# MLP of a decoder block: two sweeps, both by seven products, with weight sums made by accumulating DMA

## The chip, the core and the metric

The kernel runs on one core of a Trainium2 chip. The metric is the device time of one execution in microseconds (us). The kernel before was run three times; its median is the time that a changed kernel is held against.

## The reference

One decoder block on 512 rows of 2048 features: RMSNorm, a combined input projection, a gated delta rule and differential attention side by side, an output projection with a residual, and then the part that the change is about, the MLP, and a final RMSNorm:

```
h = h + mix @ w_o                                  # (512, 2048)
u = rms_norm(h, mlp_norm)
hid = square(relu(u @ w_up))                       # w_up (2048, 8192)
h = h + hid @ w_down                               # w_down (8192, 2048)
out = rms_norm(h, final_norm)
```

All inputs and the output are float32.

## The kernel before

Every large matrix product is made in fp32r by three matmuls: each operand is split into a rounded `hi` (ScalarE, line 147) and the rest `lo` (VectorE, line 149), and hi x hi, hi x lo and lo x hi are accumulated in PSUM. `parts` does this for a weight tile of 128 x 1024 that `load_w` has brought into a slot; slots come from pools by tag, so many for each (`BUFS`, line 43: six `raw`, three `hi`, three `lo`). All loads go through SP's queue in the order of the program. The Tile framework orders the instructions of each engine and sets the semaphores; each engine then takes its queue in order.

The MLP starts at line 947. The hidden width of 8192 is cut into 16 blocks of 512 (`NBLK`). `to_feature_major` makes the split, transposed activations `uT`: 16 tiles of 128 features x 512 rows. `up_first` makes the first block's hidden values, `up_steps` those of each later block, in four column tiles, with 512-column matmuls (`cols_steps`, lines 204 to 206); `squared_relu` writes them.

The down projection of a block is made by seven products instead of eight (a scheme of Winograd's kind): the block's hidden values, 512 x 512, and each 512 x 1024 piece of `w_down` are cut into four quarters. `seven_steps` makes the seven factors of the hidden values from sums and differences of quarters and splits each with `two`. `block_steps` goes over two column halves `p`; in each it loads four quarters of `w_down`, makes four combinations of them on VectorE (lines 864, 870, 878, 884), splits seven tiles, runs seven products (`product`, lines 835 to 837: 12 matmuls of 512 columns each, into two PSUM banks) and adds banks into the rows of h (lines 850, 852), which stay in SBUF all the time. The last block is done without the scheme (`plain_steps`).

The loop at line 996 weaves three streams: the down products of block b, the up projection of blocks b + 1 and b + 2, and the factors of block b + 1. So 360 matmuls belong to one turn, 192 up and 168 down.

Of the kernel before, what the change touches and what calls it, by code (L numbers as in the profile page):

```python
# [31 lines left out]
def hybrid_block(ctx: ExitStack, tc: tile.TileContext, x, attn_norm, w_in, conv_w, a_log, dt_bias,  # L32
# [10 lines left out]
    BUFS = {"p": 10, "x": 2, "w": 8, "m": 2, "u": 16, "raw": 6, "hi": 3, "lo": 3}  # L43
# [750 lines left out]
    def half_tile():  # L794

        return big("p", [P, 2, 2, 256], nm="hf")

    def two(src):
        z = big("w", [P, 2, 2, 256], F32R, nm="op")
        A.activation(z[:, 0], src, AF.Copy)  # L800
        V.tensor_sub(z[:, 1], src, z[:, 0].bitcast(F32))
        return z[:, 0], z[:, 1]

    def seven_steps(left, f):

        a11, a21, a12, a22 = left[0][:, 0], left[0][:, 1], left[1][:, 0], left[1][:, 1]
        f["a12"] = two(a12)
        yield
        f["a11"] = two(a11)
        z = big("m", [P, 2, 2, 256], nm="s12")  # L810
        s1, s2 = z[:, 0], z[:, 1]
        V.tensor_add(s1, a21, a22)
        yield
        f["s1"] = two(s1)
        V.tensor_sub(s2, s1, a11)
        yield
        f["s2"] = two(s2)
        s4 = s1
        V.tensor_sub(s4, a12, s2)
        yield  # L820
        f["s4"] = two(s4)
        s3 = s2
        V.tensor_sub(s3, a11, a21)
        yield
        f["s3"] = two(s3)
        yield
        f["a22"] = two(a22)
        yield

    def product(bank, fac, wts, first, last_):  # L830
        (ah, al), (bh, bl) = fac, wts
        for k in range(2):
            for t in range(2):
                st = slice(t * P, (t + 1) * P)
                T.matmul(bank[t], lhsT=ah[:, k, st], rhs=bh[:, k, :], start=first and k == 0, stop=False, skip_group_check=True)  # L835
                T.matmul(bank[t], lhsT=ah[:, k, st], rhs=bl[:, k, :], start=False, stop=False, skip_group_check=True)  # L836
                T.matmul(bank[t], lhsT=al[:, k, st], rhs=bh[:, k, :], start=False, stop=last_ and k == 1, skip_group_check=True)  # L837

    def block_steps(f, w, row0, rows):

        for p in range(2):
            def quarter(i, j):
                r0, c0 = row0 + 256 * i, 1024 * j + 512 * p
                return load_w(w[r0:r0 + 256, c0:c0 + 512].rearrange("(k p) n -> p k n", p=P), [P, 2, 512])

            def add(bank, half, cg, op=ALU.add):
                for t in range(2):
                    dst = rows[2 * half + t][cg]
                    if op == ALU.add:
                        V.tensor_add(dst, bank[t], dst)  # L850
                    else:
                        V.tensor_sub(dst, dst, bank[t])

            b21, b11, b12, b22 = quarter(1, 0), quarter(0, 0), quarter(0, 1), quarter(1, 1)
            Y = [bank(), bank()]
            product(Y, f["a12"], parts(b21, 2), True, True)
            add(Y, 0, p)
            yield
            X = [acc(), acc()]
            product(X, f["a11"], parts(b11, 2), True, False)  # L860
            add(X, 0, p)
            yield
            t1 = b11
            V.tensor_sub(t1, b12, b11)
            Z = [acc(), acc()]
            product(Z, f["s1"], parts(t1, 2), True, False)
            add(Z, 1, p + 2)
            yield
            t2 = t1
            V.tensor_sub(t2, b22, t1)  # L870
            product(X, f["s2"], parts(t2, 2), False, False)
            add(X, 0, p + 2)
            yield
            product(Z, f["s4"], parts(b22, 2), False, True)
            add(Z, 0, p + 2)
            yield
            t3 = b12
            V.tensor_sub(t3, b22, b12)
            product(X, f["s3"], parts(t3, 2), False, True)
            add(X, 1, p)  # L880
            add(X, 1, p + 2)
            yield
            t4 = b21
            V.tensor_sub(t4, t2, b21)
            Y = [bank(), bank()]
            product(Y, f["a22"], parts(t4, 2), True, True)
            add(Y, 1, p, ALU.subtract)
            yield
# [57 lines left out]

    def up_unit(u):
        return split(w_up[0, u * 256:(u + 1) * 256, 0:512].rearrange("(k p) n -> p k n", p=P), [P, 2, 512])
# [3 lines left out]
    uT = to_feature_major(h, rstd, g_mlp)  # L952
    NBLK = DFF // 512

    def up_steps(b, j, left):
        z = half_tile()
        for k in range(2):
            po = sps()
            yield from cols_steps(po, w_up[0], (4 * b + 2 * j + k) * P, uT, tag="x")
            squared_relu(z, k, po)  # L960
        left.append(z)

    def squared_relu(z, k, po):
        r = big("m", [P, 512], nm="relu")
        A.activation(r, po, AF.Relu)
        A.activation(z[:, :, k, :], r.rearrange("p (i s) -> p i s", i=2), AF.Square)

    def up_first():

        po = [acc() for _ in range(4)]  # L970
        for u in range(KD // 2):
            hi, lo = up_unit(u) if u else first
            for j in range(2):
                k = 2 * u + j
                ah, al = uT[k]
                for c in range(4):
                    st = slice(c * P, (c + 1) * P)
                    T.matmul(po[c], lhsT=hi[:, j, st], rhs=ah, start=k == 0, stop=False)
                    T.matmul(po[c], lhsT=hi[:, j, st], rhs=al, start=False, stop=False)
                    T.matmul(po[c], lhsT=lo[:, j, st], rhs=ah, start=False, stop=k == KD - 1)  # L980
        for j in range(2):
            z = half_tile()
            for k in range(2):
                squared_relu(z, k, po[2 * j + k])
            lefts[0].append(z)

    def up(b, j):
        return up_steps(b, j, lefts[b]) if b < NBLK else iter(())

    lefts = [[] for _ in range(NBLK)]  # L990
    facs = [{} for _ in range(NBLK)]
    up_first()
    floor.clear()
    run(seven_steps(lefts[0], facs[0]))
    run(up(1, 0))
    for b in range(NBLK - 2):
        down = block_steps(facs[b], w_down[0], 512 * b, h)
        for p in range(2):
            ups = up(b + 1, 1) if p == 0 else up(b + 2, 0)
            fac = seven_steps(lefts[b + 1], facs[b + 1]) if p == 1 else iter(())  # L1000
            for i in range(7):
                next(down)
                next(fac, None)
                if i % 2 == 0:
                    next(ups, None)
            run(ups)


    down = block_steps(facs[NBLK - 2], w_down[0], 512 * (NBLK - 2), h)
    ups = up(NBLK - 1, 1)  # L1010
    for i in range(7):
        next(down)
        if i % 2 == 0:
            next(ups, None)
    run(ups)
    lft = lefts[NBLK - 1]
# [94 lines left out]
```

## Time and profile before

| | |
|---|---|
| median of three runs | 2282.1 us (2281.64 to 2282.75) |
| profiled execution, its own time | 2282.81 us |
| span of the profiled execution | 2281.1 us |
| granted TensorE clock, mean | 0.997 |
| PE / weight loads / VectorE / ScalarE / POOL busy | 98% / 82% / 67% / 39% / 2% |
| DMA moved | 249.67 MB, mean 109 GB/s |
| first MLP matmul, last part | about 956 us to 2273 us from the span's start |

The profile is of one execution, and its span is the time from the first to the last instruction on the core; the time of that execution is 1.7 us more. Matmuls overlap, so the duration in a matmul's row is longer than the step from one start to the next.

### The profile page before, as it was taken

How to read it: one execution, taken by the hardware profiler on the slowest of the kernel's cores; microseconds unless marked ns; L12 is line 12 of the kernel's file. 1: busy time of each engine (PE TensorE's matmuls, PEld its weight loads, DVE VectorE, ACT ScalarE, POOL GpSimd, SP SyncE). 2: the span in 40 equal slices, each digit the busy share in tenths (PEclk: the TensorE clock that was granted, in tenths of full speed). 3: DMA queues.
4: the chain of work that ended last, by engine and by line, in shares of the span. 5: the costliest groups of instructions: out<-in, count | busy, mean ns of one | idle time of the engine just before them, and what ended most of it. 6: DMA issues, size and time to landing. Idle time of an engine off the chain costs nothing.

```text
span 2281.1 us, 27449 instructions
## 1 busy us (share of the span) xinstructions
PE 2245.4 (98%) x10649; PEld 1864.8 (82%) x10649; DVE 1523.3 (67%) x2338; ACT 887.8 (39%) x1444; POOL 55.5 (2%) x85
## 2 busy tenths in 40 slices
PE   8999999999999999999999999999999999999998
PEld 7988777778888788788888888888888888888887
DVE  5467787863355623437787687777778778777776
ACT  5233434432344523433344343343334334434343
POOL 0000100100000000000000000000000000000000
PEclk9999999999999999999999999999999999999999
DMA  8433333433232434233333333232332333323332
GB/s 282 141 111 95 109 97 96 117 92 110 85 95 88 139 92 151 83 105 98 109 93 119 95 99 113 93 123 90 98 115 93 115 98 95 118 93 120 93 127 95
DMA packets 288570, 249.67 MB, mean 109 GB/s; under 512 B 17300, under 2 KB 229560, under 8 KB 288440
## 3 DMA queue, kind: packets, MB, share of 16 engines
q1 hardware_dynamic: 287952, 247.72, 35.3%
q8 instruction: 83, 1.36, 0.3%
q14 instruction: 47, 0.39, 0.1%
q10 hardware_dynamic: 488, 0.21, 0.0%
HBM read 236.86 MB, written 11.03 MB: 109 GB/s over the span
## 4 chain that ended last, share of the span: by engine, by line
PE 90%; DVE 7%; ACT 1%; issue 1%; DMA 1%; POOL 0%; SPq 0%; ACTq 0%; POOLq 0%; DVEq 0%
PE s L206 10%; PE s L204 10%; PE s L205 10%; PE acc L837 6%; PE acc L836 6%; PE acc L835 6%; PE acc L204 5%; PE acc L205 4%; PE acc L206 4%; PE acc L220 3%; PE acc L221 3%; PE acc L222 3%; PE s L837 2%; PE s L836 2%; PE s L835 2%; DVE X L520 2%
## 5 line engine op out<-in xcount | busy, mean ns | idle before, releaser
L149 DVE TENSOR_TENSOR lo<-raw,hi 128x1024 fp32r<-128x1024 f32 (+2 forms) x370 | 443.9, 1200 | 342.3 <-ACT hi L147 337.5
L147 ACT ACTIVATE hi<-raw 128x1024 fp32r<-128x1024 f32 (+2 forms) x370 | 384.5, 1040 | 674.5 <-PE acc L205 136.7
L204 PE MATMUL s<-u,hi 128*128 128x512 f32 x960 | 373.4, 389 | 0.0
L205 PE MATMUL s<-u,hi 128*128 128x512 f32 x960 | 373.4, 389 | 0.0
L206 PE MATMUL s<-u,lo 128*128 128x512 f32 x960 | 373.4, 389 | 0.0
L149 DVE TENSOR_TENSOR lo<-x,hi 128x1024 fp32r<-128x1024 f32 x120 | 146.7, 1223 | 181.0 <-ACT hi L147 181.0
L204 PE MATMUL acc<-u,hi 128*128 128x512 f32 x640 | 260.6, 407 | 0.8 <-DVE dvl L679 0.6
L205 PE MATMUL acc<-u,hi 128*128 128x512 f32 x640 | 251.6, 393 | 0.0
L206 PE MATMUL acc<-u,lo 128*128 128x512 f32 x640 | 250.7, 392 | 0.0
L147 ACT ACTIVATE hi<-x 128x1024 fp32r<-128x1024 f32 x120 | 127.5, 1062 | 315.0 <-PE s L205 226.2
L836 PE MATMUL acc<-lo,op 128*128 128x512 f32 x600 | 233.4, 389 | 0.0
L837 PE MATMUL acc<-hi,op 128*128 128x512 f32 x600 | 233.4, 389 | 0.0
L835 PE MATMUL acc<-hi,op 128*128 128x512 f32 x600 | 233.1, 389 | 0.0
L850 DVE TENSOR_TENSOR h<-acc,h 128x512 f32<-128x512 f32 x360 | 232.2, 685 | 0.6 <-PE acc L837 0.5
L205 PEld LDWEIGHTS s<-u,hi 128*128 128x128 f32 x960 | 180.2, 188 | 37.4
L206 PEld LDWEIGHTS s<-u,lo 128*128 128x128 f32 x960 | 180.2, 188 | 37.4
L204 PEld LDWEIGHTS s<-u,hi 128*128 128x128 f32 x960 | 180.2, 188 | 37.4
L220 PE MATMUL acc<-hi,u 128*128 128x512 f32 (+2 forms) x384 | 144.7, 379 | 7.6 <-ACT hi L147 5.9
L204 PEld LDWEIGHTS acc<-u,hi 128*128 128x128 f32 x640 | 120.7, 189 | 25.0 <-DVE dvl L679 1.0
L206 PEld LDWEIGHTS acc<-u,lo 128*128 128x128 f32 x640 | 120.4, 188 | 25.3
L221 PE MATMUL acc<-lo,u 128*128 128x512 f32 (+2 forms) x384 | 140.5, 366 | 0.2 <-DVE lo L149 0.2
L222 PE MATMUL acc<-hi,u 128*128 128x512 f32 (+2 forms) x384 | 140.6, 366 | 0.0
(266 smaller groups left out, 3228.2 us busy)
## 6 DMA issues: line engine op xcount, KB each, us to landing
raw<-in_w_down_dram SPq DMA_DIRECT2D x128, 512.0 KB, 5.6
x<-in_w_up_dram SPq DMA_DIRECT2D x120, 512.0 KB, 4.2
raw<-in_w_in_dram SPq DMA_DIRECT2D x96, 512.0 KB, 3.9
raw<-in_w_o_dram SPq DMA_DIRECT2D x32, 512.0 KB, 3.8
raw<-in_w_in_dram SPq DMA_DIRECT2D x16, 384.0 KB, 8.3
w<-in_xt_dram SPq DMA_DIRECT2D x8, 512.0 KB, 8.5
p<-in_x_dram SPq DMA_DIRECT2D x8, 512.0 KB, 10.0
raw<-in_x_dram SPq DMA_DIRECT2D x8, 512.0 KB, 3.6
```

The lines of the kernel that those rows point to most:

```text
L147: A.activation(hi, raw, AF.Copy)
L149: floor["lo"] = V.tensor_sub(lo, raw, hi.bitcast(F32))
L204: T.matmul(po, lhsT=hi[:, j, :], rhs=ah, start=k == 0, stop=False)
L205: T.matmul(po, lhsT=hi[:, j, :], rhs=al, start=False, stop=False)
L206: T.matmul(po, lhsT=lo[:, j, :], rhs=ah, start=False, stop=k == KD - 1)
L220: T.matmul(o, lhsT=ah[:, st], rhs=bh, start=k == 0, stop=False)
L221: T.matmul(o, lhsT=ah[:, st], rhs=bl, start=False, stop=False)
L222: T.matmul(o, lhsT=al[:, st], rhs=bh, start=False, stop=k == KD - 1)
L835: T.matmul(bank[t], lhsT=ah[:, k, st], rhs=bh[:, k, :], start=first and k == 0, stop=False, skip_group_check=True)
L836: T.matmul(bank[t], lhsT=ah[:, k, st], rhs=bl[:, k, :], start=False, stop=False, skip_group_check=True)
L837: T.matmul(bank[t], lhsT=al[:, k, st], rhs=bh[:, k, :], start=False, stop=last_ and k == 1, skip_group_check=True)
L850: V.tensor_add(dst, bank[t], dst)
```

## The change

The MLP is made in two sweeps instead of one woven loop.

- **Up sweep.** Blocks 1 to 15 of the up projection are made by seven products too. The activations are cut in halves of rows (256) and of features (1024): `uh` holds the split tiles by halves, `uf` unsplit ones, and `u_factors` makes three of the seven factors in new tiles and a fourth in the place of the low half of `uh`. `up_product` takes 128 x 128 pieces of the weights as the stationary operand and 256 rows as the moving one: 48 matmuls of 256 columns for each product.
- **Factors by way of DRAM.** `seven_steps` makes the down projection's factors for each block as before, but `keep` stores each, split, in DRAM (512 KB), on SP's queue, for the last two blocks on POOL's. The rows of h are stored too (`hscr`) and brought back (`rows_back`).
- **Down sweep.** `block_steps` now handles a group of blocks, [0], [1 to 3], ..., [10 to 12], [13, 14], in one PSUM accumulation for each product, and adds into h once for a group. `recall` loads each factor once for a group, for both column halves.
- **Weight combinations.** The signs are moved to the factors, so that all four combinations of weights are sums. Two are made by VectorE (`sums`), two by `add_in`: a DMA issued from POOL that adds the quarter (0, 1) from DRAM onto a `raw` tile in SBUF, once it has been split for its first product.
- The tag `raw` has nine slots instead of six, and the scratch for dynamic DMA is 2048 instead of 1024.

The core of the diff (the functions taken out are those printed above):

```diff
-    BUFS = {"p": 10, "x": 2, "w": 8, "m": 2, "u": 16, "raw": 6, "hi": 3, "lo": 3}
+    BUFS = {"p": 10, "x": 2, "w": 8, "m": 2, "u": 16, "raw": 9, "hi": 3, "lo": 3}
...
+    def pair_of(src, tag):
+        z = big(tag, [P, 2, 2, 256], F32R, nm="op")
         A.activation(z[:, 0], src, AF.Copy)
         V.tensor_sub(z[:, 1], src, z[:, 0].bitcast(F32))
+        return z
+    fscr = {}
+    def keep(b, name, src):
+        z = pair_of(src, "w")
+        fscr[b, name] = dp.tile([P, 1024], F32, name=f"f_{name}_{b}")
+        E = nc.sync if b < NBLK - 2 else G
+        E.dma_start(out=fscr[b, name], in_=z.bitcast(F32).rearrange("p a k s -> p (a k s)"))
+    def negated_less(out, a, b):
+        V.scalar_tensor_tensor(out, a, -1.0, b, op0=ALU.mult, op1=ALU.subtract)
+    def seven_steps(b, left):
...
+        keep(b, "a11", a11)
+        yield
+        keep(b, "a12", a12)
+        V.tensor_sub(s1, a21, a22)
...
+        keep(b, "s3", s2)
+        yield
...
+    def recall(b, name):
+        z = big("w" if name in ("a12", "a22") else "u", [P, 2, 2, 256], F32R, nm="fac")
+        with tc.issue_after(last_load[0].ins):
+            last_load[0] = nc.sync.dma_start(out=z.bitcast(F32).rearrange("p a k s -> p (a k s)"), in_=fscr[b, name])
+        return z[:, 0], z[:, 1]
+    def add_in(raws, srcs, k):
+        for z, src in zip(raws, srcs):
+            G.dma_start(out=z.rearrange("p (k n) -> p k n", k=k), in_=src.rearrange("(k p) n -> p k n", p=P), accum_op=ALU.add)
+    def sums(a, b):
+        for x1, x2 in zip(a, b):
+            V.tensor_add(x1, x1, x2)
+    def product(bank, facs, wts, first, last_):
+        for n, ((ah, al), raw) in enumerate(zip(facs, wts)):
+            bh, bl = parts(raw, 2)
+            for k in range(2):
+                for t in range(2):
+                    st = slice(t * P, (t + 1) * P)
+                    head, tail = first and n == 0 and k == 0, last_ and n == len(facs) - 1 and k == 1
+                    T.matmul(bank[t], lhsT=ah[:, k, st], rhs=bh[:, k, :], start=head, stop=False, skip_group_check=True)
+                    T.matmul(bank[t], lhsT=ah[:, k, st], rhs=bl[:, k, :], start=False, stop=False, skip_group_check=True)
+                    T.matmul(bank[t], lhsT=al[:, k, st], rhs=bh[:, k, :], start=False, stop=tail, skip_group_check=True)
...
+        def quarter(i, j, tags=("raw",) * 3):
+            return [load_w(z.rearrange("(k p) n -> p k n", p=P), [P, 2, 512], tag=t) for z, t in zip(srcs(i, j), tags)]
...
+        t1 = quarter(0, 0)
+        fa = factor("a11")
+        X = [acc(), acc()]
+        product(X, fa, t1, True, False)
+        add_in(t1, srcs(0, 1), 2)
+        add(X, 0, p)
+        yield
+        b21 = quarter(1, 0, ("x", "x", "m"))
+        fa = factor("a12")
+        Y = [bank(), bank()]
+        product(Y, fa, b21, True, True)
+        add(Y, 0, p)
+        yield
+        fa = factor("s1")
+        Z = [acc(), acc()]
+        product(Z, fa, t1, True, False)
+        add(Z, 1, p + 2)
+        yield
+        t3 = quarter(1, 1)
+        fa = factor("s2")
+        sums(t1, t3)
+        product(X, fa, t1, False, False)
+        add(X, 0, p + 2, ALU.subtract)
+        yield
+        product(Z, factor("s4"), t3, False, True)
+        add_in(t3, srcs(0, 1), 2)
+        add(Z, 0, p + 2, ALU.subtract)
+        yield
+        fa = factor("s3")
+        product(X, fa, t3, False, True)
+        add(X, 1, p, ALU.subtract)
+        add(X, 1, p + 2)
+        yield
+        fa = factor("a22")
+        sums(t1, b21)
+        Y = [bank(), bank()]
+        product(Y, fa, t1, True, True)
+        add(Y, 1, p)
+        yield
...
+    uh, uf = [], [[], []]
...
+            z = big("u", [P, 2, 2, 256], F32R, nm="uh")
+            pv, sc = pt.rearrange("p (i s) -> p i s", i=2), g_mlp[:, k:k + 1]
+            A.activation(z[:, :, 0, :], pv, AF.Identity, scale=sc)
+            V.scalar_tensor_tensor(z[:, :, 1, :], pv, sc, z[:, :, 0, :].bitcast(F32), op0=ALU.mult, op1=ALU.subtract)
+            uh.append(z)
+            if k % 2 == 0:
+                uf[k // 8].append(big("w", [P, 2, 2, 256], nm="uf"))
+            A.activation(uf[k // 8][k % 8 // 2][:, k % 2], pv, AF.Identity, scale=sc)
+    for cg in range(4):
+        for t in range(NT):
+            G.dma_start(out=hscr[2 * cg + t // 2][:, t % 2, :], in_=h[t][cg])
...
+        floor.clear()
+        run(u_factors())
...
+    def u_factors():
+        for q in range(4):
+            xa, xb = uf[0][q], uf[1][q]
...
+            def put(n, src, tag):
+                o = big(tag, [P, 2, 2, 256], F32R, nm="u" + n)
+                A.activation(o[:, :, 0, :], src, AF.Copy)
+                V.tensor_sub(o[:, :, 1, :], src, o[:, :, 0, :].bitcast(F32))
+                for i in range(2):
+                    fu[n][2 * q + i] = o[:, i]
+            V.tensor_sub(s1, a21, a22)
+            put("s1", s1, "p")
+            negated_less(s2, s1, a11)
+            put("s2", s2, "p")
+            negated_less(s1, s2, a12)
+            put("s4", s1, "x" if q < 2 else "p")
+            V.tensor_add(a21, a11, a21)
+            for i in range(2):
+                k = 2 * q + i
+                fu["a11"][k], fu["a12"][k], fu["a22"][k] = uh[k][:, 0], uh[8 + k][:, 0], uh[8 + k][:, 1]
+                o = uh[k][:, 1]
+                A.activation(o[:, 0, :], a21[:, i, :], AF.Copy)
+                V.tensor_sub(o[:, 1, :], a21[:, i, :], o[:, 0, :].bitcast(F32))
+                fu["s3"][k] = o
+            yield
+    def up_product(bank, name, wts, first, last_):
+        for n, raw in enumerate(wts):
+            bh, bl = parts(raw, 4)
+            for j in range(4):
+                k = 4 * n + j
+                ah, al = fu[name][k][:, 0, :], fu[name][k][:, 1, :]
+                for c in range(2):
+                    dst, st = bank[:, c * 256:(c + 1) * 256], slice(c * P, (c + 1) * P)
+                    head, tail = first and k == 0 and c == 0, last_ and k == 7
+                    T.matmul(dst, lhsT=bh[:, j, st], rhs=ah, start=head, stop=False, skip_group_check=True)
+                    T.matmul(dst, lhsT=bh[:, j, st], rhs=al, start=False, stop=False, skip_group_check=True)
+                    T.matmul(dst, lhsT=bl[:, j, st], rhs=ah, start=False, stop=tail, skip_group_check=True)
+    def up_steps(b, left):
...
+            return [w_up[0, 1024 * i + 512 * n:1024 * i + 512 * n + 512, c0:c0 + 256] for n in range(2)]
+        def quarter(i, j):
+            return [load_w(z.rearrange("(k p) n -> p k n", p=P), [P, 4, 256]) for z in srcs(i, j)]
...
+        e1, e2 = (big("w", [P, 2, 512], nm="e") for _ in range(2))
+        x1, p5, u2, u3 = e1[:, 0, :], e1[:, 1, :], e2[:, 0, :], e2[:, 1, :]
+        t1 = quarter(0, 0)
+        X = acc()
+        up_product(X, "a11", t1, True, False)
+        add_in(t1, srcs(0, 1), 4)
+        A.activation(x1, X, AF.Copy)
+        yield
...
+        t3 = quarter(1, 1)
+        sums(t1, t3)
+        up_product(X, "s2", t1, False, False)
+        A.activation(u2, X, AF.Copy)
+        yield
+        up_product(Z, "s4", t3, False, True)
+        add_in(t3, srcs(0, 1), 4)
+        V.tensor_add(c12, Z, u2)
...
+        up_product(X, "s3", t3, False, True)
...
+        sums(t1, b21)
+        Y = bank()
+        up_product(Y, "a22", t1, True, True)
+        V.tensor_sub(c21, Y, u3)
...
+    left = up_first()
+    for b in range(1, NBLK):
+        fac, nxt = seven_steps(b - 1, left), []
+        for _ in up_steps(b, nxt):
+            next(fac, None)
+        run(fac)
+        left = nxt
+    last_fac = four_steps(NBLK - 1, left)
...
+    def rows_back(cgs):
+        for cg in cgs:
+            for i in range(2):
+                with tc.issue_after(last_load[0].ins):
+                    last_load[0] = nc.sync.dma_start(out=hb[2 * cg + i], in_=hscr[2 * cg + i])
+    groups = [[0]] + [[b, b + 1, b + 2] for b in range(1, NBLK - 3, 3)] + [[NBLK - 3, NBLK - 2]]
+    for g in groups:
+        f = {}
         for p in range(2):
+            down = block_steps(g, f, p, w_down[0], h)
+            if g is groups[0]:
+                rows_back((p, p + 2))
+            if g is groups[-1] and p == 1:
+                break
+            for _ in down:
+                next(last_fac, None)
...
-    nc = bacc.Bacc("TRN2", target_bir_lowering=False, num_devices=1, dynamic_dma_scratch_size=1024)
+    nc = bacc.Bacc("TRN2", target_bir_lowering=False, num_devices=1, dynamic_dma_scratch_size=2048)
```

## Rows read from the trace of the kernel before

**Rows 1.** The page's first part: busy us of each engine, share, instructions.
```profile
PE 2245.4 (98%) x10649; PEld 1864.8 (82%) x10649; DVE 1523.3 (67%) x2338; ACT 887.8 (39%) x1444; POOL 55.5 (2%) x85
```

**Rows 2.** Busy time by stretch, columns as its first line says.
```profile
core 0: us, PE busy (x) PEld busy (x) DVE busy (x) ACT busy (x) POOL busy (x), PEclk, DMA share, GB/s
2.00:30.00 28.00, 19.27 (x97) 18.58 (x98) 19.34 (x35) 18.75 (x31) 0.86 (x5) 1.00 0.99 349
966.00:1010.00 44.00, 44.00 (x196) 36.24 (x195) 15.51 (x16) 17.05 (x24) 0.00 (x0) 1.00 0.33 98
1300.00:1382.00 82.00, 82.00 (x363) 67.92 (x362) 61.60 (x73) 31.70 (x37) 0.00 (x0) 1.00 0.32 103
```

**Rows 3.** PE's waits over the whole span: us in total, times, longest.
```profile
PE acc L220 <- ACT hi L147: 5.9, 2, 4.5
PE s L114 <- DVE lp L112: 4.7, 1, 4.7
```

**Rows 4.** Timeline of PE, 512-column matmuls: start us, duration us, engine, line.
```profile
1500.12 0.39 PE L204 MATMUL s<-u,hi 128*128 128x512 f32 x1
...
1505.56 0.39 PE L835 MATMUL acc<-hi,op 128*128 128x512 f32 x1
```

**Rows 5.** Timeline of PE, 272-column matmuls.
```profile
84.77 0.29 PE L220 MATMUL acc<-hi,u 128*128 128x272 f32 x1
...
92.21 0.29 PE L222 MATMUL acc<-hi,u 128*128 128x272 f32 x1
```

**Rows 6.** Timeline of PE, 256-column matmuls.
```profile
646.74 0.28 PE L733 MATMUL s<-dvh,at 128*128 128x256 f32 x1
646.85 0.28 PE L734 MATMUL s<-dvl,at 128*128 128x256 f32 x1
646.97 0.28 PE L735 MATMUL s<-dvh,at 128*128 128x256 f32 x1
647.09 0.40 PE L220 MATMUL acc<-hi,u 128*128 128x512 f32 x1
```

**Rows 7.** Groups by line and shape on VectorE: count, busy us, mean ns.
```profile
L149 DVE TENSOR_TENSOR lo<-raw,hi 128x1024 fp32r<-128x1024 f32 x346 | 422.8, 1223 | 304.8 <-ACT hi L147 300.0 <-PE s L625 4.7
L850 DVE TENSOR_TENSOR h<-acc,h 128x512 f32<-128x512 f32 x360 | 232.2, 685 | 0.6 <-PE acc L837 0.5
L864 DVE TENSOR_TENSOR raw<-raw,raw 128x1024 f32<-128x1024 f32 x30 | 36.6, 1219 | 0.0
L801 DVE TENSOR_TENSOR op<-hf,op 128x512 fp32r<-128x512 f32 x49 | 32.3, 684 | 0.0
L812 DVE TENSOR_TENSOR s<-hf,hf 128x512 f32<-128x512 f32 x15 | 10.4, 692 | 0.0
```

**Rows 8.** The same on ScalarE.
```profile
L147 ACT ACTIVATE hi<-raw 128x1024 fp32r<-128x1024 f32 x346 | 365.7, 1058 | 629.7 <-PE acc L205 136.7 <-PE s L205 120.6 <-PE acc L837 116.3
L966 ACT ACTIVATE hf<-relu 128x512 f32<-128x512 f32 x64 | 40.4, 634 | 1.9
L965 ACT ACTIVATE relu<-s 128x512 f32<-128x512 f32 x60 | 34.7, 578 | 2.8 <-PE s L206 2.8
L800 ACT ACTIVATE op<-hf 128x512 fp32r<-128x512 f32 x49 | 30.9, 632 | 29.3 <-PE acc L837 27.7
```

**Rows 9.** DMA issues by line: count, KB each, median us from issue to landing.
```profile
raw<-in_w_down_dram SPq DMA_DIRECT2D x128, 512.0 KB, 5.6
x<-in_w_up_dram SPq DMA_DIRECT2D x120, 512.0 KB, 4.2
p<-in_x_dram SPq DMA_DIRECT2D x8, 512.0 KB, 10.0
raw<-in_x_dram SPq DMA_DIRECT2D x8, 512.0 KB, 3.6
```

**Rows 10.** Groups by line and shape on POOL.
```profile
L128 POOL TENSOR_TENSOR rstd<-rs,mhalf 128x1 f32<-128x1 f32 x24 | 13.7, 571 | 1644.2 <-DVE rs L127 1644.2
L128 POOL TENSOR_TENSOR fac<-rs,mhalf 128x8 f32<-128x8 f32 x4 | 8.0, 1993 | 144.2 <-DVE rs L127 144.2
```

More of the change, by code (lines that the diff above doesn't have):

```diff
@@ L822, in seven_steps @@
-        s3 = s2
-        V.tensor_sub(s3, a11, a21)
+        keep(b, "s2", s2)
         yield
-        f["s3"] = two(s3)
+        negated_less(s1, s2, a12)
+        keep(b, "s4", s1)
         yield
-        f["a22"] = two(a22)
+        keep(b, "a22", a22)
+        V.tensor_add(s2, a11, a21)
         yield
-    def product(bank, fac, wts, first, last_):
-        (ah, al), (bh, bl) = fac, wts
-        for k in range(2):
-            for t in range(2):
[L834 to L888, printed above, removed]
@@ new lines, in seven_steps, with four_steps @@
+        keep(b, "s3", s2)
+        yield
+    def four_steps(b, left):
+        for j in range(2):
+            for i in range(2):
+                keep(b, f"a{i + 1}{j + 1}", left[j][:, i])
+                yield
[4 more added lines that the diff above has]
+        return z[:, 0], z[:, 1]
@@ new lines, in block_steps, with srcs, factor, add @@
+    def block_steps(bs, f, p, w, rows):
+        def srcs(i, j):
+            c0 = 1024 * j + 512 * p
+            return [w[512 * b + 256 * i:512 * b + 256 * i + 256, c0:c0 + 512] for b in bs]
+        def quarter(i, j, tags=("raw",) * 3):
+            return [load_w(z.rearrange("(k p) n -> p k n", p=P), [P, 2, 512], tag=t) for z, t in zip(srcs(i, j), tags)]
+        def factor(name):
+            if name not in f:
+                f[name] = [recall(b, name) for b in bs]
+            return f[name]
+        def add(bank, half, cg, op=ALU.add):
+            for t in range(2):
+                dst = rows[2 * half + t][cg]
+                if op == ALU.add:
+                    V.tensor_add(dst, bank[t], dst)
+                else:
+                    V.tensor_sub(dst, dst, bank[t])
+        t1 = quarter(0, 0)
[37 more added lines that the diff above has]
+        yield
@@ L944, in hybrid_block @@
     run(rows_steps(po, w_o[0], 3 * 512, 512, mix, by_token=4, done=finish))
+    NBLK = DFF // 512
     def up_unit(u):
@@ L974, in up_first @@
                 k = 2 * u + j
-                ah, al = uT[k]
+                ah, al = uh[k][:, :, 0, :], uh[k][:, :, 1, :]
                 for c in range(4):
@@ L983, in up_first @@
             for k in range(2):
[L984 to L997, printed above, removed]
-        for p in range(2):
[L999 to L1006, printed above, removed]
@@ L1009, in hybrid_block @@
[L1009 to L1016, printed above, removed]
-    fac = [[two(lft[j][:, i]) for i in range(2)] for j in range(2)]
+                r = big("m", [P, 512], nm="relu")
+                A.activation(r, po[2 * j + k], AF.Relu)
+                A.activation(z[:, :, k, :], r.rearrange("p (i s) -> p i s", i=2), AF.Square)
```

95 lines of the change are left out of this document (65 added, 30 removed).

## Prediction

> **What bounds the kernel now.** I read the page's part 1 first, then the same kind of figures for single stretches, then the waits of TensorE, then the rows of single matmuls, and last the prices of what the other engines and the DMA queues do.
>
> The page's first part [rows 1] says that PE is busy 98% of 2281.1 us and VectorE 67%. A busy PE may still be a slow one, so the stretches come next [rows 2]. In the middle of the MLP, 1300 to 1382, PE is busy for all of 82 us, at a granted clock of 1.00 (the 2.4 GHz level), with 363 matmuls; VectorE has 61.60 us, ScalarE 31.70, and the DMA engines stand at 0.32. The list of PE's waits [rows 3] is short and its longest entries are 5.9 and 4.7 us over the whole span, from lines ahead of the MLP. So from about 966 to 2273 the time is a number of matmuls times the step from one matmul's start to the next, and nothing else ends last.
>
> That step is not the duration in a row. A 128x512 row says 0.39 us, but 24 of them start between 1500.12 and 1505.56 [rows 4]: 0.2267 us each. The dense run of 128x272 matmuls starts 59 of them between 84.77 and 92.21 [rows 5]: 0.1261 us each. The line through both gives 0.419 ns a column and 12 ns besides, so a 128x256 matmul should step at 0.1261 - 16 x 0.000419 = 0.1194 us. The only 256-wide fp32r matmuls in the kernel stand alone among wide ones: three take 646.74 to 647.09 [rows 6], 0.117 each. I use 0.1194 and keep 0.117 as a bound.
>
> **The change part by part.** *Matmuls of the up projection.* Before, one of the 15 blocks has 4 x 16 x 3 = 192 matmuls of 512 columns: 192 x 0.2267 = 43.5 us. After, it has 7 products x 2 tiles x 4 x 2 x 3 = 336 of 256 columns: 336 x 0.1194 = 40.1 us. That is 3.4 us a block, 51.1 us over 15 (64 at 0.117). An eighth of the columns goes away, but the 12 ns that each matmul pays besides its columns are paid 336 times and not 192, which eats 1.7 us a block. The Trainium skill, "TensorE: Matmul & The Clock Gate", section "Back-to-back issue gap", gives N / 2.4 + 2.5 ns, so 215.8 and 109.2 ns; by it the block would fall from 41.4 to 36.7 us and the sum would be 71 us, but the rows show 226.7 ns for 512 columns, so the rows decide.
>
> *Matmuls of the down projection.* Seven products for 15 blocks are 15 x 2 x 7 x 12 = 2520 matmuls of 512 columns before and after, and the last block's 192 stay. Nothing is gained here on PE. What goes is VectorE work: 32 additions into h for each block become 32 for each group of up to three.
>
> *VectorE and ScalarE in the new sweeps.* By their rows [rows 7, 8], an up block costs VectorE 14 `lo` at 1.22, 4 sums at 1.22, 4 results at 0.69, 7 halves of `pair_of` at 0.69 and 4 factor sums at 0.69: 32.3 of 40.1 us. ScalarE has 14 `hi` at 1.06, 4 copies and 4 Relus at 0.58, 11 more at 0.63: 26 us. A column half of a three-block group costs VectorE 21 x 1.22 + 6 x 1.22 + 16 x 0.69 = 44 of 21 x 12 x 0.2267 = 57 us. Both stay below PE: 81% and 77%, where it is 75% now [rows 2]. I charge nothing for them as totals; what they cost as delay is in the next part.
>
> *The accumulating DMAs.* This is the part that no row shows: the kernel before has no DMA from POOL and none that adds. `add_in` is issued when `parts` has read the tile, and the tile's next `parts` waits for it. How much time lies between? A unit is one raw tile's matmuls: 24 x 0.1194 = 2.87 us up, 12 x 0.2267 = 2.72 us down. `hi` and `lo` have three slots, and ScalarE's `hi` mostly waits for PE to give one back, so unit n is split at (n - 2) units, plus 1.06 + 1.22 us and some 0.9 for a neighbour on VectorE and the handovers. A tile that is wanted again m units later has to be split (2.3 us) by n + m. The window is (m + 2) units - 5.5 us. For `t3`, whose two products follow each other, that is 6.0 us in the up sweep (m = 2), 8.1 in a group of three, 5.4 in the group of two, 2.7 in the group of one. For `t1` one product lies between: 11.7 up, 5.4 in the group of one, more elsewhere.
>
> How long from POOL's issue to landing? The 512 KB loads now take 3.6 to 5.6 us, and 10.0 when the queue is full at 0.99 DMA share [rows 9, 2]. An add must read its destination too: 512 KB at 349 GB/s is another 1.5 us (estimate from [rows 2]). What POOL needs to start one is bounded by its cheap and dear instructions, 0.57 and 1.99 us [rows 10]. Lowest: 3.6 + 0.6 = 4.2 us. Highest: 10.0 + 1.5 + 2.0 = 13.5. I take 4.2 + 1.5 + 0.9 = 6.6, since the load that most resembles it, w_up's, has 4.2, with the DMA engines busier than now but not full (below). So `t3` is late by 0.6 us in 15 up blocks (9 us), by 3.9 twice and `t1` by 1.2 twice in the group of one (10.2), by 1.2 twice in the group of two (2.4), by nothing in the four groups of three: 21.6 us. What is late next is `a22`: ScalarE and VectorE take their queues in order, so its split stands behind that of the tile in waiting, unless the order of issue puts it ahead, which would add two units (5.7 us) to the window.
>
> *DMA volume.* An up block moves 6 loads, 4 adds and 7 stores of 512 KB: 8.9 MB in 40.1 us, 222 GB/s; with the adds' second read 275. A three-block group moves 18 loads, 12 adds and 21 recalls: 26.7 MB in 114 us, 234 GB/s, with second reads 290. Now it is 103, and 349 is what the engines gave at 0.99 [rows 2]. It fits, at some 80%. SP takes its queue in order, and the stores of `keep` stand there between loads and wait for `pair_of`; nine `raw` slots against six used by an up block are the cover. Without it the loads behind would be late by up to one store, 4 us.
>
> *Seams.* `u_factors` puts some 25 us on VectorE (36 instructions of up to 0.69) beside `up_first`, where it has 15.51 of 44 us [rows 2]: 28 us are free. ScalarE's 16 `uf` copies meet 17.05 of 44. I take 5 us for both (0 to 25). At the change of sweeps the first group wants some 8 MB in 7 x 2.72 = 19 us, and 8 MB at 349 GB/s are 23 us; some of it is there early, and I take 3. The stores of h and the last block's four factors go past SP on POOL's queue and nothing near waits for them.
>
> **The sum.** -51.1 + 21.6 + 8 = -21.5 us. The profiled execution took 2282.81 us for its span of 2281.1; the median of the runs is 2282.1. The forecast against that median is 2261 us, 0.9% faster. With every wait at its low end (4.2 us to landing: 3 us in the group of one; seams 0) it is 2234; the likeliest case alone spans 2236 to 2277.
>
> **The rivals.**
>
> *The adds are late (slower).* Each us by which a landing passes 6.0 us costs 15 us in the up sweep and some 6 in the small groups. 51 - 8 = 43 us are used up when 15(L - 6.0) + 2(L - 2.7) + 4(L - 5.4) = 43, at L = 7.6 us: beyond it the change loses. At 9 us: 45 + 19.8 + 7.2 + 7.2 (groups of three) = 79, so 2318 us. At 13.5 us, where `t1` is late as well, some 2460. For it speak the 10.0 us of a full queue; against it that 222 GB/s is no full queue, and that `a22` may be issued ahead.
>
> *POOL gets no room beside VectorE (slower).* VectorE will be busy 81% of an up block. If POOL's work on an add (1.2 us, between its rows) ran only in the 19% that VectorE leaves, it would take 6 us, L would be 11.4, and the sum 81 + 29 + 12 + 26 = 148 us of waits: 2387. No row bears this out, since POOL and VectorE meet on nothing like it. The Trainium skill, "SBUF — State Buffer", section "Who interferes with whom", says that descriptors of POOL's DMAs are starved while VectorE runs a two-port mode and advises against such DMAs there; it excepts the tensor_tensor form, which is what this kernel runs.
>
> *The DMA engines fill.* If adds and loads together got only 250 GB/s, an up block would need 44 us, the change's gain in the up sweep would be gone (15 x 4 us), and with the other waits the time about 2320.
>
> *Narrow matmuls don't pay (the change does not do what it says).* A weight load lasts 67.92 us / 362 = 188 ns [rows 2]; were it the bound at 256 columns, a block would take 336 x 0.188 = 63 us and the kernel 2577. The run at 272 columns and 0.1261 us speaks against it.
>
> **How the numbers follow.** Forecast, L up to 7.4 us or `a22` ahead: 0.55. Gain and waits cancel, L 7.4 to 7.8: 0.09. Adds late: 0.21. POOL starved: 0.06. DMA engines full: 0.06. Narrow matmuls at 188 ns: 0.03. 0.2% is 4.6 us, about what a measurement of this kernel can tell from no change. So faster 0.55, same 0.09, slower 0.36. The range leaves out 0.05 below 2236 and, above 2330, the starved, the 188 ns and the worst of the late case, 0.13.
>
> **What would show it.** Right: matmuls of 256 columns step at 0.117 to 0.12 us in the up sweep, an up block takes 41 to 42 us, PE's waits there are below 1.5 us a block and name ScalarE's `hi` of the `s3` product; groups of three run at 114 us. Wrong: waits of several us a block on that line, with the add's landing above 7.6 us; a step near 0.19; or SP's loads landing late throughout.

## The result, and the profile after

The changed kernel takes 2450.61 us (median of four runs, 2442.51 to 2455.54) against 2282.43 us before, measured beside it: a ratio of 1.0733, interval 1.0703 to 1.0763. It is 7.3% slower, 168 us, where 21 us less had been forecast. The profiled execution took 2442.51 us, with a span of 2440.7 us and a mean granted clock of 0.969.

The page's first part of the kernel after answers to [rows 1]:

```profile
PE 2283.5 (94%) x12809; PEld 1980.8 (81%) x12809; DVE 1518.4 (62%) x2236; ACT 1017.6 (42%) x1630; POOL 219.0 (9%) x232
```

PE is no longer the engine that is always busy: 94% of a longer span. VectorE has fallen to 62%, ScalarE stands at 42%, POOL at 9%: no other engine has become the bound. So something makes PE wait, and the stretches say where. The view of stretches of the kernel after answers to [rows 2]: the up sweep, one block and two short stretches in it, the change of sweeps (two rows), most of the groups of three, the end.

```profile
core 0: us, PE busy (x) PEld busy (x) DVE busy (x) ACT busy (x) POOL busy (x), PEclk, DMA share, GB/s
1010.00:1758.00 748.00, 664.72 (x5016) 645.79 (x5015) 460.91 (x494) 365.20 (x493) 80.29 (x67) 0.93 0.68 181
...
1308.00:1359.00 51.00, 45.30 (x345) 43.79 (x344) 30.96 (x34) 24.61 (x34) 5.14 (x4) 0.93 0.68 176
1331.00:1343.00 12.00, 7.53 (x35) 6.69 (x36) 3.61 (x4) 3.58 (x4) 1.29 (x1) 0.72 0.53 122
1335.80:1340.00 4.20, 4.20 (x21) 4.20 (x21) 0.00 (x0) 0.47 (x1) 0.00 (x0) 0.50 1.08 225
...
1758.00:1770.00 12.00, 8.39 (x21) 5.43 (x22) 8.97 (x12) 5.25 (x7) 1.18 (x3) 0.72 1.03 414
1770.00:1850.00 80.00, 65.47 (x266) 51.94 (x265) 57.65 (x65) 23.73 (x23) 7.80 (x8) 0.91 0.89 292
1850.00:2275.00 425.00, 413.10 (x1786) 337.73 (x1786) 296.19 (x305) 156.22 (x148) 53.15 (x45) 0.99 0.76 215
2275.00:2430.00 155.00, 145.61 (x614) 116.10 (x613) 104.16 (x128) 57.11 (x77) 11.41 (x12) 0.98 0.54 159
```

A stretch's loss is its length less its matmuls at their full step. For 512 columns that is 0.2267 us [rows 4]. For 256 columns the runs below give it: 4919 in 590 us, 0.1199 us. Up sweep: 748 - 5016 x 0.1199 = 146 us lost (some 3 us too much, as 24 of these matmuls are already 512 columns wide). Change of sweeps: 12 - 21 x 0.2267 = 7 and 80 - 266 x 0.2267 = 20. Groups of three: 425 - 1786 x 0.2267 = 20. End: 155 - 614 x 0.2267 = 16. These make 209 us; with 51 us less matmul work the span should grow by 158, and it grew by 160.

So seven tenths of the loss is in the up sweep. PE's waits there in the kernel after (in all, times, longest), which answer to [rows 3]:

```profile
PE acc L1104 <- ACT hi L147: 53.8, 32, 3.4
PE acc L1106 <- DVE lo L149: 27.1, 45, 0.8
```

The first line is where the prediction looked for trouble: `hi` of the tile that an add has gone into. But named waits are 81 of the 146 us. The rest is seen in the timeline of PE in one block of the kernel after (start, duration, what it waited for), to be held against [rows 6]:

```profile
1330.47 0.28 PE L1105 MATMUL acc<-us,hi 128*128 128x256 f32 x1
1330.59 0.28 PE L1106 MATMUL acc<-us,lo 128*128 128x256 f32 x1
1334.14 0.41 PE L1104 MATMUL acc<-uh,hi 128*128 128x256 f32 x1 [3.27 <-ACT hi L147]
...
1335.40 0.58 PE L1106 MATMUL acc<-uh,lo 128*128 128x256 f32 x1 [0.64 <-DVE lo L149]
1335.78 0.42 PE L1104 MATMUL acc<-uh,hi 128*128 128x256 f32 x1
...
1340.05 0.41 PE L1106 MATMUL acc<-uh,lo 128*128 128x256 f32 x1
1340.64 0.58 PE L1104 MATMUL acc<-uh,hi 128*128 128x256 f32 x1 [0.17 <-ACT hi L147]
...
1341.89 0.38 PE L1106 MATMUL acc<-uh,lo 128*128 128x256 f32 x1 [0.51 <-DVE lo L149]
1342.12 0.28 PE L1104 MATMUL acc<-uh,hi 128*128 128x256 f32 x1
```

`s4` ends at 1330.59; the first matmul of `s3` comes at 1334.14, after 3.27 us of waiting. Then 20 steps take 1335.78 to 1340.05, 0.2135 us each and not 0.120, and from 1342.12 the step is 0.12 again. The granted clock of 1335.8 to 1340 is 0.50 in the windows above, the 1.2 GHz level. A wait of three microseconds thus costs some 3 us more after its end: the 27 matmuls from 1334.14 to 1342.12 take 7.98 us, where 27 full steps are 3.24 us and the short waits among them 1.32. Over the up sweep, 421 steps of 0.20 to 0.23 us make 40 of the 65 us that no wait names; most of the rest is in the steps beside the waits.

Why the tile is late stands in POOL's timeline of the same block (both adds of a pair belong to one `add_in`):

```profile
1306.62 1.29 POOL L857 DMA_DIRECT2D raw<-in_w_up_dram  x1 [7.83 <-issue]
1325.45 1.29 POOL L857 DMA_DIRECT2D raw<-in_w_up_dram  x1 [17.54 <-DVE lo L149]
1333.26 1.29 POOL L857 DMA_DIRECT2D raw<-in_w_up_dram  x1 [6.53 <-issue]
1349.03 1.28 POOL L857 DMA_DIRECT2D raw<-in_w_up_dram  x1 [14.47 <-DVE lo L149]
1357.43 1.29 POOL L857 DMA_DIRECT2D raw<-in_w_up_dram  x1 [7.12 <-issue]
```

and in ScalarE's, where `hi` of a tile starts when the add into it has landed:

```profile
1313.38 2.01 ACT L147 ACTIVATE hi<-raw 128x1024 fp32r<-128x1024 f32 x2 [4.93 <-DMA raw<-in_w_up_dram]
...
1333.03 1.06 ACT L147 ACTIVATE hi<-raw 128x1024 fp32r<-128x1024 f32 x1 [6.75 <-DMA raw<-in_w_up_dram]
1339.53 2.00 ACT L147 ACTIVATE hi<-raw 128x1024 fp32r<-128x1024 f32 x2 [5.44 <-DMA raw<-in_w_up_dram]
```

The first add into `t3` goes out at 1325.45 and has landed by 1333.03. The second tile was split by 1326.2, yet its add goes out at 1333.26, after 6.53 us in which POOL waited for nothing that the profile shows ("issue"), and 0.23 us after that. It has landed by 1339.53: 14.1 us after the first was issued. The same happened to `t1` (1306.62, landed 1313.38). POOL's waits of the up sweep in the kernel after count 20 such cases:

```profile
POOL raw L857 <- DVE lo L149: 483.9, 36, 17.6
POOL raw L857 <- issue: 125.9, 20, 7.8
```

That list undercounts. By the landing times in the trace, the second add goes out 0.32 to 0.38 us after the first has landed in all 30 pairs of the up sweep; in nine of them the list names another releaser than "issue". In the down sweep no add waits for the landing of another; the adds of one group of three mostly go out 2.7 us apart. A `w_up` tile is added as 512 rows of 1 KB (4 for each partition), a `w_down` tile as 256 rows of 2 KB.

One add in flight does not land badly. The DMA issues of the kernel after (count, size, median us to landing), which answer to [rows 9]:

```profile
raw<-in_w_up_dram POOLq DMA_DIRECT2D x60, 512.0 KB, 6.6
fac<-f_s SPq DMA_DIRECT2D x60, 512.0 KB, 10.3
raw<-in_w_down_dram POOLq DMA_DIRECT2D x60, 512.0 KB, 9.1
```

So the theory: **the second add of a pair in the up sweep cannot be issued while the first is in flight, since the scratch for dynamic DMA, 2048, has room for one of them; its lateness eats the lead of the splits, PE waits for the next added tile, and the clock falls.** (The lead is how far a tile's split is ahead of the product that reads it; the wait of POOL is called the hold below.) The rival: a landing of 6 to 9 us in a window of 6 is late by itself, whatever POOL does. A second rival: VectorE or the DMA engines are too full.

### The profile page after: what moved, and what is told of

Its sections match the earlier page's. It is cut to its first block, busy times and chain, and to the rows that moved or that the text cites. A ratio compares the mean times of both kernels' runs of the same rounds, so it can differ in the third digit from the quotient of the medians.

```text
span 2440.7 us, 32868 instructions
## 1 busy us (share of the span) xinstructions
PE 2283.5 (94%) x12809; PEld 1980.8 (81%) x12809; DVE 1518.4 (62%) x2236; ACT 1017.6 (42%) x1630; POOL 219.0 (9%) x232
## 4 chain that ended last, share of the span: by engine, by line
issue 47%; PE 38%; DVE 7%; POOL 4%; DMA 2%; ACT 1%; POOLq 0%; SPq 0%; ACTq 0%; DVEq 0%
PE acc L204 4%; PE acc L205 4%; PE acc L206 4%; POOL raw L857 4%; PE acc L220 3%; PE acc L221 3%; PE acc L222 3%; DVE X L520 2%; PE s L222 2%; PE s L220 2%; PE s L221 2%; DVE lo L149 1%; DVE X L521 1%; DMA raw<-in_w_down_dram 1%; DVE cv L415 1%
## 5 line engine op out<-in xcount | busy, mean ns | idle before, releaser
L149 DVE TENSOR_TENSOR lo<-raw,hi 128x1024 fp32r<-128x1024 f32 (+2 forms) x550 | 661.0, 1207 | 621.9 <-ACT hi L147 612.1
L147 ACT ACTIVATE hi<-raw 128x1024 fp32r<-128x1024 f32 (+2 forms) x550 | 569.4, 1045 | 971.8 <-DMA raw<-in_w_up_dram 237.9
L870 PE MATMUL acc<-hi,fac 128*128 128x512 f32 x600 | 239.5, 402 | 32.2 <-ACT hi L147 32.2
L871 PE MATMUL acc<-lo,fac 128*128 128x512 f32 x600 | 240.9, 402 | 9.4 <-DVE lo L149 9.4
L872 PE MATMUL acc<-hi,fac 128*128 128x512 f32 x600 | 238.7, 398 | 0.0
L1106 PE MATMUL acc<-us,lo 128*128 128x256 f32 x720 | 206.8, 287 | 6.8 <-DVE lo L149 6.7
L1104 PE MATMUL acc<-us,hi 128*128 128x256 f32 x720 | 204.6, 284 | 1.3 <-ACT hi L147 1.3
L1104 PE MATMUL acc<-uh,hi 128*128 128x256 f32 x480 | 155.6, 324 | 52.5 <-ACT hi L147 52.5
L1105 PE MATMUL acc<-us,hi 128*128 128x256 f32 x720 | 204.3, 284 | 0.0
L1106 PE MATMUL acc<-uh,lo 128*128 128x256 f32 x480 | 156.5, 326 | 20.4 <-DVE lo L149 20.4
L1105 PE MATMUL acc<-uh,hi 128*128 128x256 f32 x480 | 152.2, 317 | 0.0
L220 PE MATMUL acc<-hi,u 128*128 128x512 f32 (+2 forms) x384 | 144.6, 379 | 6.2 <-ACT hi L147 6.2
L1106 PEld LDWEIGHTS acc<-us,lo 128*128 128x128 f32 x720 | 138.6, 192 | 10.7 <-DVE lo L149 10.3
```

What stands on the lines that cost most here:

```text
L147: A.activation(hi, raw, AF.Copy)
L149: floor["lo"] = V.tensor_sub(lo, raw, hi.bitcast(F32))
L220: T.matmul(o, lhsT=ah[:, st], rhs=bh, start=k == 0, stop=False)
L1104: T.matmul(dst, lhsT=bh[:, j, st], rhs=ah, start=head, stop=False, skip_group_check=True)
L1105: T.matmul(dst, lhsT=bh[:, j, st], rhs=al, start=False, stop=False, skip_group_check=True)
L1106: T.matmul(dst, lhsT=bl[:, j, st], rhs=ah, start=False, stop=tail, skip_group_check=True)
```

## The experiments

The first four kernels were measured beside 2283.3 us for the kernel before.

**Scratch 2560.** The order of instructions on each engine is the same.

```diff
-    nc = bacc.Bacc("TRN2", target_bir_lowering=False, num_devices=1, dynamic_dma_scratch_size=2048)
+    nc = bacc.Bacc("TRN2", target_bir_lowering=False, num_devices=1, dynamic_dma_scratch_size=2560)
```

> Only the scratch for dynamic DMA grows, from 2048 to 2560 bytes; every engine's order of instructions is unchanged. Theory A (ring): in the up sweep the second add of a pair sits on POOL until the first has landed, 6.5 us, because the descriptors of both do not fit; with 2560 they do. POOL then issues it 2.9 us after the first, t1's second half lands early enough that the lead of the split over PE is kept, and an up block falls from 50.4 us to 43 to 46: 2340 to 2390 us. Rival B (landing): what counts is the 6 to 8 us of the transfer itself at 0.69 DMA share, or POOL waits for the landing whatever the room; then at most 20 us are won: 2430 to 2455.

Measured: 2353.44 us, 1.0308 (1.0289 to 1.0327), 97 us less than the kernel after, for one number. POOL's timeline of this kernel:

```profile
1309.44 1.28 POOL L857 DMA_DIRECT2D raw<-in_w_up_dram  x1 [17.78 <-DVE lo L149]
1311.18 1.29 POOL L857 DMA_DIRECT2D raw<-in_w_up_dram  x1 [0.45 <-DVE lo L149]
1332.78 2.59 POOL L857 DMA_DIRECT2D raw<-in_w_up_dram  x2 [20.31 <-DVE lo L149]
```

Pairs go out together: no second add of the up sweep waits for the landing of the first any more, and no "issue" entry is left. But the stretch 1010 to 1650 of this kernel still loses 640 - 4897 x 0.1199 = 53 us:

```profile
1010.00:1650.00 640.00, 607.55 (x4897) 598.25 (x4897) 447.61 (x480) 357.33 (x478) 77.01 (x62) 0.98 0.77 203
```

and its PE waits there name the same two lines:

```profile
PE acc L1106 <- DVE lo L149: 17.7, 25, 0.8
PE acc L1104 <- ACT hi L147: 14.8, 14, 3.5
```

Its adds of `w_up` take 8.8 us (median) to land, two being in flight, against the window of 6.0 us that the prediction gives `t3`: 15 x 2.8 = 42 us. So the rival seems right as well, for this part: the hold is there, and so is a window that is too short. The runs below test the second.

**Scratch 1536.** The same edit with 1536.

> The scratch shrinks to 1536 bytes, the order of instructions is unchanged. Theory A: the up sweep, where only one add fits already, stays at 50 us a block; in the down sweep, where three adds are issued 2.7 us apart now, the third is held, and a group of three grows from 121 us by 2 to 15 us: 2455 to 2510 us. Rival B: no change anywhere, 2450 us.

Measured: 2448.75 us, 1.0726 (1.0704 to 1.0747), the time of the kernel after. POOL's waits of the down sweep (1850 to 2290) in this kernel, where the kernel after has 0.2 us in one:

```profile
POOL raw L857 <- DVE lo L149: 303.8, 25, 25.8
POOL raw L857 <- issue: 52.4, 11, 7.5
```

So the smaller scratch holds back adds of 256 rows too, as the theory has it, but the time did not follow: 1850 to 2275 holds 1781 matmuls here and 1786 in the kernel after. Perhaps the windows of a group of three, 8 us and more, hide the hold; no run tests that. The rise that was expected did not come.

**No adds.** The four calls of `add_in` are left out, so that two of the four weight combinations lack a summand; all else stays.

```diff
-        add_in(t1, srcs(0, 1), 2)
...
-        add_in(t3, srcs(0, 1), 2)
...
-        add_in(t1, srcs(0, 1), 4)
...
-        add_in(t3, srcs(0, 1), 4)
```

> All accumulating DMAs are left out (so two of the four combinations of weights lack a summand); all else is as in the changed kernel. Theory A and B both: the waits of the up sweep go with the adds, a block takes 40.5 to 41.5 us, a group of three 114 to 115, what is left of the excess is the change of sweeps: 2245 to 2275 us. Rival C (VectorE at 80% and SP's queue lose the lead by themselves): waits stay, 2350 us or more.

Measured: 2246.26 us, 0.9839 (0.9819 to 0.9859). Everything that the change costs beyond its gain hangs on the adds, but for some 14 us (51 us of matmuls gone, 37 us of time). Their bytes are gone too, so this run does not tell the hold from the landing. The up sweep of this kernel runs with PE busy throughout:

```profile
1010.00:1600.00 590.00, 590.00 (x4919) 590.00 (x4918) 454.75 (x485) 360.11 (x484) 2.19 (x4) 1.00 0.50 169
```

**`a22` ahead of `s3`.** The window of `t3` becomes two units longer; scratch 2048. In the up sweep, its core (the down sweep likewise):

```diff
+        sums(t1, b21)
+        Y = bank()
+        up_product(Y, "a22", t1, True, True)
+        yield
         up_product(X, "s3", t3, False, True)
...
-        yield
-        sums(t1, b21)
-        Y = bank()
-        up_product(Y, "a22", t1, True, True)
         V.tensor_sub(c21, Y, u3)
```

> In both sweeps the a22 product is made ahead of the s3 product, so that t3's add has two units more (5.7 us up, 2.7 to 8.1 us down); the scratch stays at 2048. Theory A: the second half of t3 lands 14 us after the first is issued, against four units, 11.5 us, so t3's wait (some 4.6 us and 2.9 us at half clock per up block) shrinks to 1 to 3 us, t1's stays: 2340 to 2380 us. Rival C: no change, 2440 to 2455.

Measured: 2348.43 us, 1.0284 (1.0267 to 1.0302): 102 us less than the kernel after, with the hold still there (again in all 30 pairs). The first row is its up sweep, the second 480 us of its down sweep that hold most groups of three and the start of the last group:

```profile
1010.00:1681.60 671.60, 627.28 (x4992) 616.99 (x4991) 457.25 (x491) 357.45 (x489) 80.30 (x67) 0.97 0.74 198
1792.00:2272.00 480.00, 473.88 (x2081) 391.69 (x2080) 350.48 (x364) 185.67 (x177) 57.17 (x48) 0.99 0.78 227
```

The same 480 us, counted from the end of the up sweep, in the kernel with scratch 2560:

```profile
1771.00:2251.00 480.00, 464.10 (x1977) 377.45 (x1978) 332.07 (x344) 176.30 (x168) 54.69 (x46) 0.98 0.76 220
```

Each remedy alone gives back some 100 of the 168 us, but not in the same places. The new order loses 671.6 - 4992 x 0.1199 = 73 us in the up sweep, half of what the kernel after loses there, and 480 - 2081 x 0.2267 = 8 us in the down sweep, where the larger scratch alone still loses 480 - 1977 x 0.2267 = 32. What the larger scratch gives back is in the up sweep (146 to 53 us). Neither theory alone explains the up sweep; the next kernels put the two together (beside 2282.87 us before).

**Both: scratch 2560 and `a22` ahead of `s3`.**

> Scratch of 2560 bytes and a22 ahead of s3 together. Theory A (the adds' landing against the time until the tile is wanted is all that is lost in the up sweep): with both, t1 has 11.5 us for 7 to 8, t3 four units as well, so the up sweep's excess of 52 us (larger scratch alone) and 66 us (order alone) falls to 10 to 25 us: 2295 to 2315 us. Rival C (what is left comes from VectorE and SP, not from the adds): both remedies overlap, 2335 to 2350 us.

Measured: 2273.72 us, 0.9958 (0.9944 to 0.9972), less than either side expected. The stretches of this kernel: the up sweep, one block, the first 112 us of the down sweep, and 480 us of it that hold most groups of three and the start of the last group.

```profile
1010.00:1600.00 590.00, 590.00 (x4919) 590.00 (x4918) 453.58 (x484) 357.01 (x482) 76.79 (x62) 1.00 0.81 220
...
1308.00:1348.00 40.00, 40.00 (x336) 40.00 (x335) 30.93 (x33) 24.48 (x33) 5.13 (x4) 1.00 0.81 223
1607.60:1720.00 112.40, 93.79 (x370) 72.78 (x369) 76.71 (x88) 36.33 (x39) 12.37 (x12) 0.92 0.92 300
1720.00:2200.00 480.00, 475.09 (x2084) 391.82 (x2083) 351.48 (x365) 187.43 (x179) 57.08 (x48) 0.99 0.77 225
```

The 336 matmuls of a block take 40.0 us, the whole up sweep is without loss, and the clock stays at 1.00. The adds are still there and take 8.4 us to land; the DMA engines stand at 0.81, VectorE at 77%. What is left is the change of sweeps above all: 112.4 - 370 x 0.2267 = 29 us, at a DMA share of 0.92; the stretch after it loses 8.

**Up sums on VectorE.** In the up sweep the quarter (0, 1) is loaded by SP and added by VectorE; down sweep and scratch as in the kernel after.

```diff
+        b12 = quarter(0, 1)
...
-        add_in(t1, srcs(0, 1), 4)
+        sums(t1, b12)
...
-        add_in(t3, srcs(0, 1), 4)
+        sums(t3, b12)
```

> In the up sweep alone the quarter (0, 1) is loaded into raw slots by SP once and added by VectorE (4 more instructions of 1.22 us a block), the adds by DMA are gone there; the down sweep, its order and the scratch are as in the changed kernel. Theory A: VectorE then has 37.2 of 40.3 us and no add is waited for; a block takes 40.5 to 43 us, 2290 to 2335 us. Rival C: VectorE at 92% loses its lead over PE, or eight of nine raw slots held by one block delay the loads, and the block stays at 46 us or more: 2370 us or more.

Measured: 2299.56 us, 1.0072 (1.0052 to 1.0092). The stretches of this kernel:

```profile
1010.00:1600.00 590.00, 590.00 (x4919) 590.00 (x4918) 518.78 (x543) 361.23 (x484) 2.18 (x4) 1.00 0.58 196
1720.00:2200.00 480.00, 461.41 (x1969) 374.86 (x1968) 332.50 (x344) 175.51 (x167) 54.75 (x46) 0.98 0.76 220
```

No loss in the up sweep, with VectorE busy 88%; 480 - 1969 x 0.2267 = 34 us of loss in the groups of three and the start of the last group, which still have their adds and their old order.

**Up sums on VectorE, and `a22` ahead of `s3` in the down sweep, with 2560.**

> As the run before, with a22 ahead of s3 in the down sweep and a scratch of 2560. Theory A: the down groups' excess of some 6 us each and a part of that of the small groups goes: 15 to 30 us below the run before. Rival: the change of sweeps is bound by the DMA engines (0.96 share there with the larger scratch), and less than 10 us are won.

Measured: 2273.13 us, 0.9957 (0.9942 to 0.9971). Its groups of three hold 2083 matmuls in 1720 to 2200, as many as the kernel with both remedies. So the 26 us between the last two runs are those of the window of `t3` in the down sweep. The larger scratch, which differs as well, does not explain them: alone it leaves 32 of the 34 us of this stretch, and the new order alone leaves 8. And it makes no difference whether the sums of the up sweep are made by DMA or by VectorE, as long as nobody waits.

**Smaller groups at the ends.** Both remedies, and two blocks in the first group and in the two last.

```diff
-    groups = [[0]] + [[b, b + 1, b + 2] for b in range(1, NBLK - 3, 3)] + [[NBLK - 3, NBLK - 2]]
+    groups = [[0, 1]] + [[b, b + 1, b + 2] for b in range(2, 11, 3)] + [[11, 12], [13, 14]]
```

> As the run with both remedies, but the groups of blocks are [0, 1], three of three, [11, 12], [13, 14] instead of [0], four of three, [13, 14]. Theory A: in the group of one an add that lands after some 9 us at a full queue meets a window of 2.7 us, twice, and two units of its product are too few; with two blocks the window is 5.4 and the first group has twice the matmuls over which its loads are spread: 10 to 25 us less than the run with both remedies. Rival (the change of sweeps is bound by bytes): two blocks need twice the bytes at once, no gain or a loss of up to 15 us.

Measured: 2265.6 us, 0.9924 (0.9904 to 0.9943): 0.8% less than the kernel before, and 8 us less than both remedies without it, where 10 to 25 had been expected. The first 110 us of the down sweep in this kernel:

```profile
1609.50:1720.00 110.50, 100.79 (x415) 80.27 (x414) 73.64 (x83) 39.62 (x42) 14.17 (x14) 0.95 0.93 301
```

110.5 - 415 x 0.2267 = 16 us of loss: some 12 of the 29 are back, with the DMA engines as full as before. 3 us of that are lost again in 1720 to 2200, which holds 2069 matmuls in place of 2084. That more matmuls for each byte at the start made the gain fits the rows, but is argued: the last groups were changed in the same run.

## Why the prediction was wrong

- **What bounds the kernel before: right.** Every loss above is a wait or a slow step of PE.
- **Matmuls of the up projection: right.** 0.1194 us a matmul and 40.1 us a block were predicted; 0.1199 and 40.0 came, where nothing waits.
- **VectorE and ScalarE: right.** 32.3 and 26 us a block were predicted; 30.93 and 24.48 stand in the block with both remedies. VectorE at 88% did not cost anything either.
- **The landing of an add: right for one, by luck in part; wrong for two.** 6.6 us was predicted, as 4.2 + 1.5 + 0.9, and 6.6 is the median in the up sweep. It holds there because only one add is in flight at a time, and that comes from the hold, which the prediction did not have. With two in flight (scratch 2560) the median is 8.8.
- **The step that failed** is in "The accumulating DMAs": "`add_in` is issued when `parts` has read the tile". In the up sweep the second add of every pair is issued only when the first has landed, with POOL idle for 5 to 8 us before it. It had then landed 12 to 16 us after the first went out (14.1 in the block shown), where the prediction had 6.6 us from its own issue and windows of 6.0 for `t3` and 11.7 for `t1`. So the term of 9 us for the up blocks came out as 146. Shown by scratch 2560 (the holds go, and 97 us with them, at an unchanged order of instructions) and by 1536 (holds come in the down sweep). That it is the number of rows that fills the scratch is argued from the three sizes and the two shapes, not measured.
- **The window of `t3` had a lead in it that was not there.** The prediction has "unit n is split at (n - 2) units"; in the block shown, the first tile of `s4` is split when PE is due to read it (its add goes out at 1325.45, `s4` runs from 1324.9), because the late `t1` held up the splits behind it. VectorE's first and last `lo` in the piled-up work show it:

```profile
1314.47 1.23 DVE L149 TENSOR_TENSOR lo<-raw,hi 128x1024 fp32r<-128x1024 f32 x1 [4.03 <-ACT hi L147]
...
1323.82 2.35 DVE L149 TENSOR_TENSOR lo<-raw,hi 128x1024 fp32r<-128x1024 f32 x2
```

It waits for `hi` of the second `t1` tile, then works without a pause until both `t3` tiles are split at 1326.2. So `t3`'s first tile, whose add was not held at all, came 3.3 us late. By the prediction's rule that add goes out 2.5 us before `s4` starts; in most of ten blocks read from each trace it goes out 0.5 us after that start in the kernel after, some 1.1 us before it with scratch 2560, and 2.7 us before it with both remedies. So scratch 2560 gives some of the lead back, but with landings of 8.8 us the window of 6.0 stays too short, and 53 us stay lost; the new order alone lengthens the window and keeps the hold, and 73 us stay lost; with both, nothing is lost in the up sweep.

- **The price of a wait was too low.** The late case counted the waiting alone. In the block shown PE ran at a step of 0.2135 us for some 20 matmuls after a wait of 3 us; over the up sweep such steps cost 40 us. By the rival's own sum, a landing of 9 us gave 2318 us; the kernel with scratch 2560, in which adds land in 8.8 to 9.0 us and none is held, took 2353.
- **Seams: too small.** The change of sweeps was put at 3 us with "some of it is there early"; it lost 27 us, at a DMA share of 0.89 and more. Groups of three were put at no loss, with a window of 8.1 us; adds landed in 9.1 us (median) in the down sweep, and the stretch lost 20 us; the new order gave 26 us back in the down sweep.
- **DMA volume in the sweeps: right.** 0.68 to 0.81 share, and no loss in the up sweep at 0.81. No run measures the add's second read of 1.5 us by itself, but an add does cost more than its bytes: two loads more a block raise the share from 0.50 (no adds) to 0.58 (up sums on VectorE), four adds a block raise it to 0.81 (both remedies). By these shares an add takes about twice the DMA engines' time of a load of the same size (estimate).
- **The rivals.** "The adds are late" is what happened, in the up sweep by way of a hold that it didn't have. "POOL gets no room beside VectorE" is refuted: its rows are 1.28 us with VectorE at 77%, and PE does not wait. The Trainium skill, "SBUF — State Buffer", section "Who interferes with whom", makes its exception for the tensor_tensor form, and the runs agree. "The DMA engines fill" did not happen in the up sweep; at the change of sweeps they stand at 0.92 while PE waits, but small groups got 12 us back at the same share, so whether they are the bound there is open. "Narrow matmuls don't pay" is refuted by the step.

The Trainium skill, "DMA: Bandwidth & Descriptors", section "SWDGE vs HWDGE vs iDMA", says that GpSimd writes the descriptors of its DMAs into rings kept in SBUF. That two adds wait for each other at 2048 and not at 2560 agrees with rings that can be full.

With both remedies the change takes 9 us less than the kernel before, and with small groups 17, where 21 had been forecast.

Open: how many rows the scratch holds, and what is left of the loss at the change of sweeps (some 16 us with small groups).

## What to carry to other kernels

A DMA that is issued "when its buffer is ready" also needs room to be issued: look at the gap between two issues on POOL, and where it ends with the landing of the first, try a larger scratch. Count the window of an in-place add for the last DMA of a pair, and put a product between the add and its use, which here was worth as much as the scratch (102 and 97 us) and, unlike it, helped in both sweeps. Do not price a wait of PE by its length alone: in the up sweep 81 us of named waits came with a loss of 146 us, 40 of it at the lower clock.

## What the runs showed of the hardware

- Scratch for dynamic DMA: at 2048, an accumulating DMA of 512 rows of 1 KB held the next one back until it had landed (all 30 pairs of the up sweep, POOL idle for 6.4 us on average); at 2560 none did. Of 256 rows of 2 KB none was held at 2048, where the three of a group went out 2.7 us apart; at 1536 some were (11 times by POOL's list, 4.8 us on average).
- An accumulating DMA of 512 KB landed in 6.6 us (median of 60) with no other in flight, and in medians of 8.4 to 10.5 us with another in flight or in the down sweep; POOL's own row for one is 1.2 to 1.3 us.
- After a wait of 3.27 us the granted clock stood at 0.50, the 1.2 GHz level, and 256-column matmuls stepped at 0.2135 us instead of 0.1199, until some 8 us after PE had started again.
